# Fetching the rows of h: a second layout of x, a modulation copy by channel block, and earlier scores for one head pair

## The chip, the cores and the metric

The kernel runs on one core of a Trainium2 chip. The core has five engines with a queue of instructions each: TensorE (PE, with its weight loads shown as PEld), VectorE (DVE), ScalarE (ACT), GpSimd (POOL) and SyncE (SP). Each works through its own queue in order and waits on semaphores for the others. Sixteen DMA engines move data between DRAM and the on-chip memory (128 partitions); a DMA is issued by one of the engines, here mostly by SyncE, sometimes by GpSimd or ScalarE. The metric is the time of one launch in microseconds (us).

## The reference, cut to what matters

One layer of a backbone: 256 latent rows x and 256 context rows ctx, 2048 channels each. Both are normalised and modulated into h, and nearly all the rest are products of h with parts of one large matrix.

```python
mod = silu(c) @ w_mod + b_mod                 # shift, scale, gate; likewise for c_ctx
h   = layer_norm(x)   * (1 + scale)   + shift
h_c = layer_norm(ctx) * (1 + scale_c) + shift_c
aq, ak, av, az, bq, bk, bv, bz, bg, mga, mgb = split(h @ w_in)     # and the same for h_c
y_a = neighbourhood_attention(aq, ak, av, ak_c, av_c, na_rpb)       # 16 heads of 64
y_b = gated_linear_attention(bq, bk, bv, bg, and those of h_c)      # 4 heads, both directions
out = (sigmoid(mga) * ((y_a * silu(az)) @ w_br_a)
     + sigmoid(mgb) * ((y_b * silu(bz)) @ w_br_b)) @ w_out
x_new = layer_norm(alpha * x + gate * out, ln_g, ln_b)
```

The kernel never forms the values bv = h @ w_in[:, BV]. It multiplies the weights of the linear attention with the rows of h first (tile `g`) and then with that part of the matrix (tile `o`). For this it needs h with the rows on the partitions, beside the h with channels on the partitions that all other products use.

## The kernel before, in words

All products are done in a float32 form that TensorE takes at its fast rate: an operand is split into a high part (a cast on ScalarE, line 147) and a low part (a subtraction on VectorE, line 149), and three products are summed.

*Start (to about 136 us).* The rows of x and ctx are loaded, turned and normalised; the modulation is worked out per block of 128 channels (16 blocks, `mds`: scale and shift for latent and context), and h with channels on the partitions (`hhi`, `hlo`) is built block by block, together with the keys of the first seven head pairs (`kp`).

*The stream of weights.* All further weights come in units of 512 KB (352 KB for the value columns, `r_av`), in the order in which the program uses them. `load` issues the DMA on SyncE into one of four `raw` buffers, then ScalarE and VectorE split it. `load` also counts the units; a table `events` holds work that is tied to a count, and runs it as that load is written, ahead of the products of that unit. Thus the scores of the attention (`s`), the turning of its weights (`tp`) and the fetch of h rows are spread over the stream. `at(step, ...)` writes into that table.

*Attention.* `project_pair(p)` makes the keys and queries of head pair p; half of the low part of the queries is moved across partitions by a DMA that GpSimd issues (`q<-q`, line 488). `scores` multiplies them into the PSUM tile `s` (one pair of banks, so that the next scores wait until the exponentials have read it), adds the bias on VectorE (508), takes the maximum (510) and the exponentials on ScalarE (514). `read_values` (`op`) uses the result. Head pairs 0 to 5 go in groups of two, each followed by a third of the value columns (`va`, eight units); those take four PSUM banks, which the copies of the queries (483, 484, 487) have to free first. Head pair 6 is by itself: its two units are loads 37 and 38, the keys of pair 7 (`kp7`) are loads 39 and 40, its queries loads 41 and 42.

*Rows of h.* Eight blocks of 256 channels, block n at load 6 + 6n. `fetch_and_scale` issues on SyncE the modulation of the block to all partitions (`sb`, from the DRAM copy `mods`) and the four row groups of x and ctx (`xr`), and VectorE forms h from them (411, 412). One load later it is split, five loads later the two parts are stored to DRAM (`hrows`, line 425). `sb` and `xr` share two buffers (`staging`), so that a fetch waits for the stores of the block before to land; later two other tiles (`cs`, `wg`) use them as well, which is why the last block is fetched late. `mods` is written once by `store_modulation`, at about 136 us.

*The order.* Within an engine the framework's planner orders the instructions: by the order in which the program writes them, and by the time at which its own costs have their operands ready. `tc.issue_after(ins)` ties instructions behind another of the same engine.

*Later stages.* After the attention come keys, queries and gates of the linear attention (`bk`, `bq`, about 345 to 480 us), the `g` and `o` products that read `hrows` back (480 to 720), the gate `bz` with the gate column of the modulation (735 to 830), then `mga`, `pa`, `mgb`, `pb` (to 1140), the output product `wo`, and the last normalisation.

Of the kernel before, what the change touches and what calls it, by code (L numbers as in the profile page):

```python
# [8 lines left out]
F32 = mybir.dt.float32  # L9
# [7 lines left out]
P = 128  # L17
D = 2048
KT = 16
# [69 lines left out]
def tile_backbone_layer(  # L89
    ctx: ExitStack,  # L90
    tc: tile.TileContext,
    xin: bass.AP,
    cvec: bass.AP,
    wmod: bass.AP,
    bmod: bass.AP,
# [14 lines left out]
    nc = tc.nc  # L110
# [4 lines left out]
    small = ctx.enter_context(tc.tile_pool(name="small", bufs=4))  # L115
    ps = ctx.enter_context(tc.tile_pool(name="ps", bufs=1, space=PSUM))
    dram = ctx.enter_context(tc.tile_pool(name="dram", bufs=1, space=bass.MemoryType.DRAM))
    mods = dram.tile([2, 2, D], F32, name="mods")
    hrows = dram.tile([KT, P, 2, 4, P], F32, name="hrows")

    def k8(shape, name, dt=F32):
# [5 lines left out]
    def k2(shape, name, dt=F32):  # L127
        return work.tile(shape, dt, tag="k2", name=name, bufs=5)
# [7 lines left out]
    def bank(name):  # L136
        return ps.tile([P, 512], F32, tag="bank", name=name, bufs=2)

    def tiny(shape, name, bufs=4):
        return small.tile(shape, F32, tag=name, name=name, bufs=bufs)  # L140
# [4 lines left out]
    def split(hi, lo, src, after=None):  # L145
        with tc.issue_after(after[0]) if after else nullcontext():
            cast = nc.scalar.copy(hi, src)  # L147
        with tc.issue_after(after[1]) if after else nullcontext():
            sub = nc.vector.tensor_tensor(out=lo, in0=src, in1=hi.bitcast(F32), op=ALU.subtract)  # L149
        return cast.ins, sub.ins  # L150
# [79 lines left out]
    for i in range(4):  # L230
        cols = slice(P * i, P * i + P)
# [118 lines left out]
    for kt in range(KT):  # L350
# [3 lines left out]
        for p in range(K0):  # L354
# [3 lines left out]
            c = slice(P * p, P * p + P)  # L358
# [27 lines left out]
    def store_modulation():  # L386
        tp = bank("mdt")
        nc.tensor.transpose(tp[:64, :P], mds[:].rearrange("p a b k -> p (a b k)"), ident[:])
        mt = k2([64, P], "mdt")
        nc.vector.tensor_copy(mt[:], tp[:64, :P])  # L390
        nc.sync.dma_start(mods[:].rearrange("a b (k p) -> (a b k) p", p=P), mt[:])

    def staging(shape, name, dt=F32R):
        return const.tile(shape, dt, tag="staging", name=name, bufs=2)

    def rows_of_h(n):
        sb = staging([P, 2, 2, 256], f"sb{n}")
        xr = staging([P, 2, 4, P], f"xr{n}")
        b, x = sb[:].bitcast(F32), xr[:].bitcast(F32)
        cols = slice(256 * n, 256 * n + 256)  # L400

        def fetch_and_scale(dma, sub):
            with tc.issue_after(dma):
                nc.sync.dma_start(b, mods[:, :, cols].partition_broadcast(P))
                for i in range(4):
                    nc.sync.dma_start(x[:, :, i, :], xin[i, :, cols].rearrange("p (f c) -> p f c", f=2))
            for i in range(4):
                xi, s = x[:, :, i, :], i // 2
                scale, shift = (b[:, m, s, :].rearrange("p (f c) -> p f c", f=2) for m in range(2))
                with tc.issue_after(sub):  # L410
                    nc.vector.scalar_tensor_tensor(xi, xi, mvs[:, i, 0:1], scale, ALU.subtract, ALU.mult)
                nc.vector.scalar_tensor_tensor(xi, xi, rsn[:, 0, i : i + 1], shift, ALU.mult, ALU.add)

        def parts(dma, sub):
            with tc.issue_after(sub):
                split(
                    sb[:].rearrange("p a b c -> p (a b c)"),
                    xr[:].rearrange("p a b c -> p (a b c)"),
                    x.rearrange("p a b c -> p (a b c)"),
                )  # L420

        def store(dma, sub):
            with tc.issue_after(dma):
                for part, src in enumerate((b, x)):
                    nc.sync.dma_start(
                        hrows[2 * n : 2 * n + 2, :, part].rearrange("f p j c -> p f (j c)"),
                        src.rearrange("p f a b -> p f (a b)"),
                    )

        return fetch_and_scale, parts, store  # L430

    for n in range(8):
# [108 lines left out]
    def at(step, *calls):  # L541
        for fn, *args in calls:
            events.setdefault(step, []).append(lambda *_, fn=fn, args=args: fn(*args))
# [47 lines left out]
    for g in range(3):  # L591
        q = k8([P, 2, 2, 2, T], f"q{g}", F32R)
        first, second = project_pair(2 * g, q), project_pair(2 * g + 1, q)
        f0, s0, t0 = attention(2 * g, *first)
        f1, s1, t1 = attention(2 * g + 1, *second)
        n = len(loads) + 1
# [11 lines left out]
    f0, s0, t0 = attention(6, *first)  # L608
    f0()
    n = len(loads)  # L610
    at(n + 3, (s0, 0))
    at(n + 5, (s0, 1), (t0, 0))
    second = project_pair(7, q)
    f1, s1, t1 = attention(7, *second)
# [273 lines left out]
    for i in range(2):  # L888
        s = slice(4 * i, 4 * i + 4)
# [30 lines left out]
    def gate_b(c):  # L920
        z = rows_of(f"bz{c}", xh, xl, stepped=False)
        s = k4([P, 2, 512], f"sz{c}")
        yb = (yb0, yb1)[c // 2]
        for t in range(2):
            nc.scalar.activation(s[:, t, :], z[t][:], AF.Sigmoid)
            nc.vector.tensor_tensor(out=s[:, t, :], in0=s[:, t, :], in1=z[t][:], op=ALU.mult)
            y = yb[:, t, 512 * (c % 2) : 512 * (c % 2) + 512]
            nc.vector.tensor_tensor(out=s[:, t, :], in0=s[:, t, :], in1=y, op=ALU.mult)
        return s
# [48 lines left out]
    for c in range(NH):  # L978
        s = gate_b(c)
# [5 lines left out]
    for c in range(NC):  # L985
# [5 lines left out]
        sb, sig = gated(c, "b", ybh, ybl, KT)  # L991
# [46 lines left out]
    for g in range(NC - 1):  # L1038
        ops = [acc(f"wo{g}_{t}") for t in range(2)]
        for k in range(0, KT, 2):  # L1040
# [3 lines left out]
            for t in range(2):  # L1044
                for i in range(2):
                    c = slice(512 * i, 512 * i + 512)
# [68 lines left out]
    r, q = tiny([P, 1], "rr"), tiny([P, 1], "rt")  # L1115
# [14 lines left out]
    for g in range(NC):  # L1130
        cols = slice(512 * g, 512 * g + 512)
# [10 lines left out]
def _layout(inp):  # L1142
    import numpy as np

    a = {k: np.asarray(v) for k, v in inp.items()}
    f32 = np.float32
    r = {}
    r["xin"] = np.concatenate([a["x"][0].reshape(2, P, D), a["ctx"][0].reshape(2, P, D)])
    r["cvec"] = np.stack([a["c"][0].reshape(KT, P).T, a["c_ctx"].reshape(KT, P).T], axis=-1)

    wm, bm = a["w_mod"][0], a["b_mod"][0]
    cols = np.array([[D + P * k + np.arange(P), P * k + np.arange(P)] for k in range(KT)])
    w = wm.reshape(2, 8, P, 3 * D)
    r["wmod"] = np.stack([w[:, :, :, cols[k].ravel()].transpose(0, 2, 1, 3) for k in range(KT)])
    bsel = bm[cols].transpose(2, 0, 1)
    r["bmod"] = np.stack([bsel, bsel], axis=-1)
    r["wgate"] = wm[:, 2 * D :].reshape(KT, P, 2, 1024).transpose(0, 2, 1, 3)
    r["bgate"] = bm[2 * D :].reshape(1, D)

    win = a["w_in"][0]  # L1160
    r["wak"] = win[:, AK : AK + P * K0].reshape(KT, P, P * K0)
    av = np.concatenate([win[:, AV : AV + 1024], win[:, BG : BG + 32]], axis=1)
    av = av.reshape(8, 2, P, 3, AVW).transpose(3, 0, 2, 1, 4)
    r["wav"] = av.reshape(24, P, 2 * AVW)
    mats = {"w_in": win, "w_br_a": a["w_br_a"][0], "w_br_b": a["w_br_b"][0], "w_out": a["w_out"][0]}
    st = np.empty((len(UNITS), P, 1024), f32)
    for i, (_, (m, cl, k, n)) in enumerate(UNITS):
        blk = mats[m][P * k : P * (k + n)][:, cl]
        st[i] = blk.reshape(n, P, len(cl)).transpose(1, 0, 2).reshape(P, 1024)
    r["wst"] = st  # L1170

    pad = np.full((16, 15, 64, 64), NEG, f32)
    for c in range(64):
        c0 = min(max(c - 8, 0), 48)
        for kc in range(c0, c0 + 16):
            pad[:, :, c, kc] = a["na_rpb"][0][:, :, kc - c + 15]
    tab = np.empty((P, 16, 6, 64), f32)
    for rr in range(2):
        for e in range(6):
            tab[64 * rr : 64 * rr + 64, :, e, :] = pad[:, e - 2 - rr + 7].transpose(1, 0, 2)  # L1180
    r["rpb"] = tab.reshape(P, NP, 2, 384).transpose(1, 0, 2, 3)

    g2 = a["gla_w_gate2"][0]
    wg = np.zeros((4, 2, 16, 2, 512), f32)
    for d in range(2):
        wg[:, d, :, d, :] = g2[d]
    r["wg2"] = wg.reshape(P, 2, 512)
    r["bg2"] = a["gla_b_gate"][0].reshape(2, NH, P).transpose(2, 1, 0)
    r["ng"] = a["gla_norm_g"][0].reshape(4, P).T
    r["lng"] = a["ln_g"][0]  # L1190
    r["lnb"] = a["ln_b"][0]

    pos = np.arange(T)
    inv = 10000.0 ** (-np.arange(64, dtype=np.float64) / 64)
    inv = inv.astype(f32)
    ang = np.concatenate(
        [(pos // 64).astype(f32)[None, :] * inv[:, None], (pos % 64).astype(f32)[None, :] * inv[:, None]]
    ).astype(np.float64)
    r["rope"] = np.stack([np.cos(ang), -np.sin(ang), np.sin(ang)], axis=1).astype(f32)
    return {k: np.ascontiguousarray(v) for k, v in r.items()}  # L1200


_INS = [
    "xin", "cvec", "wmod", "bmod", "wgate", "bgate", "wak", "wav", "wst",
    "rpb", "wg2", "bg2", "ng", "lng", "lnb", "rope",
]

# [16 lines left out]
```

## Time and profile before

| | us |
|---|---|
| three runs | 1242.54, 1245.6, 1246.83 |
| median | 1245.6 |
| the profiled execution, its own time | 1247.71 |
| its span in the profile | 1246.0 |
| mean granted TensorE clock in it | 0.994 of full speed |
| sb fetches, median from issue to landing | 10.4 |
| xr fetches, median from issue to landing | 9.0 |
| loads of 352 KB (r_av), median from issue to landing | 4.5 |

The span is what the profiler sees of the program on the core; the profiled execution's own time has 1.7 us around it. A line like L404 is a line of the kernel before. A name as `sb<-mods` is the tile written and the one read; an "SPq" row is a DMA issue on SyncE, whose length is the time that SyncE was held by the issue, and not that of the transfer. In a row of a waits view, the bracket names how long the engine had stood still and who released it. In a windows row the columns are: stretch and length, busy time (and count) of PE, PEld, DVE, ACT and, where it worked, POOL, then the granted clock, the share of the DMA engines that was busy, and GB/s.

### The profile page before, as it was taken

To read this page: it belongs to the slowest core of one execution; us is meant where nothing else is said; L and a number is where in the kernel's file an instruction comes from. 1 tells how busy PE (TensorE), PEld (TensorE's weight loads), DVE (VectorE), ACT (ScalarE), POOL (GpSimd) and SP (SyncE) were. 2 spreads that over 40 slices of the span, in tenths; PEclk is the share of its full clock that TensorE was granted. 3 is DMA by queue.
4 is the path that set the end of the run, shared out by engine and by line. 5 is a ranking of instruction groups with operands and counts; after the bars stand their busy time and mean duration, and the time that the engine had idled before them with its cause. 6 is when DMAs were issued, how large, how long until landed. Compare 5 with 4: busy or idle time off the path is not lost.

```text
span 1246.0 us, 17116 instructions
## 1 busy us (share of the span) xinstructions
PE 1207.7 (97%) x6617; PEld 1015.1 (81%) x6617; DVE 757.5 (61%) x1114; ACT 536.9 (43%) x752; POOL 73.0 (6%) x106
## 2 busy tenths in 40 slices
PE   6999989999999999999999999999999999999997
PEld 5666889989788998888788898788888888888785
DVE  6755566666569376355543368898555554555577
ACT  4322445545456354253533364444444344444440
POOL 1000101010110101002000000000000000000111
PEclk9999989999999999999999999999999999999999
DMA  9997458787743434554645669989655556557661
GB/s 378 418 407 285 145 151 245 186 202 178 216 155 120 134 108 130 203 152 135 233 145 182 215 207 319 312 299 312 210 186 191 196 186 195 194 186 269 223 218 68
DMA packets 88993, 264.55 MB, mean 212 GB/s; under 512 B 9536, under 2 KB 22928, under 8 KB 83792
## 3 DMA queue, kind: packets, MB, share of 16 engines
q1 hardware_dynamic: 83744, 252.53, 60.3%
q0 software_dynamic: 4736, 10.37, 2.9%
q8 instruction: 52, 0.85, 0.3%
q10 hardware_dynamic: 432, 0.56, 0.1%
q14 instruction: 29, 0.24, 0.1%
HBM read 247.66 MB, written 10.52 MB: 207 GB/s over the span
## 4 chain that ended last, share of the span: by engine, by line
PE 70%; DMA 12%; DVE 10%; issue 3%; ACT 3%; SPq 2%; POOL 0%; DVEq 0%; ACTq 0%; POOLq 0%
PE bk L143 7%; PE mgb L143 7%; PE mga L143 7%; PE pb L143 7%; PE g L143 6%; PE o L143 6%; PE kp L143 6%; PE pa L143 3%; DMA wg<-in_wgate 3%; PE va L143 3%; PE bq L143 3%; PE wo L143 3%; PE az L143 2%; DMA hrows<-xr 2%; PE gp L143 2%
## 5 line engine op out<-in xcount | busy, mean ns | idle before, releaser
L149 DVE TENSOR_TENSOR l_wv<-r_wv,h_wv 128x1024 fp32r<-128x1024 f32 x32 | 39.2, 1225 | 79.8 <-ACT h_wv L147 79.6
L143 PE MATMUL o<-h_wv,gt 128*128 128x512 f32 x256 | 84.1, 391 | 0.6 <-DVE gt L149 0.6
L143 PE MATMUL g<-ah,hr 128*128 128x512 f32 x256 | 79.3, 390 | 1.1 <-DMA hr<-hrows 1.1
L143 PE MATMUL va<-h_av,hhi 128*128 128x352 f32 x192 | 64.5, 336 | 9.9 <-ACT q L487 9.9
L149 DVE TENSOR_TENSOR l_pb<-r_pb,h_pb 128x1024 fp32r<-128x1024 f32 x32 | 39.2, 1225 | 47.8 <-ACT h_pb L147 47.8
L147 ACT CAST h_wv<-r_wv 128x1024 fp32r<-128x1024 f32 x32 | 33.6, 1049 | 74.4 <-DMA r_wv<-in_wst 74.4
L143 PE MATMUL va<-h_av,hlo 128*128 128x352 f32 x192 | 63.0, 328 | 0.0
L143 PE MATMUL va<-l_av,hhi 128*128 128x352 f32 x192 | 62.9, 327 | 0.0
L149 DVE TENSOR_TENSOR l_mgb<-r_mgb,h_mgb 128x1024 fp32r<-128x1024 f32 x32 | 39.2, 1224 | 32.7 <-ACT h_mgb L147 32.5
L955 DVE SCALAR_TENSOR_TENSOR gacc<-wg,sc,gacc 128x512 f32<-128x512 f32 x64 | 46.4, 747 | 17.9 <-DMA wg<-in_wgate 17.5
L143 PEld LDWEIGHTS o<-h_wv,gt 128*128 128x128 f32 x256 | 47.8, 188 | 11.6 <-DVE gt L149 1.8
L149 DVE TENSOR_TENSOR l_mga<-r_mga,h_mga 128x1024 fp32r<-128x1024 f32 x32 | 39.1, 1223 | 28.9 <-ACT h_mga L147 28.9
L143 PEld LDWEIGHTS g<-ah,hr 128*128 128x128 f32 x256 | 47.7, 188 | 11.0 <-DMA hr<-hrows 1.3
L147 ACT CAST h_mga<-r_mga 128x1024 fp32r<-128x1024 f32 x32 | 33.8, 1055 | 49.5 <-PE mga L143 31.2
L143 PE MATMUL kp<-hhi,h_ak 128*128 128x512 f32 x128 | 52.7, 418 | 2.2 <-ACT hhi L304 2.2
L147 ACT CAST h_mgb<-r_mgb 128x1024 fp32r<-128x1024 f32 x32 | 33.6, 1054 | 47.7 <-PE mgb L143 26.1
L147 ACT CAST h_pb<-r_pb 128x1024 fp32r<-128x1024 f32 x32 | 33.7, 1053 | 43.4 <-PE pb L143 30.1
L143 PE MATMUL bz<-l_bz,hhi 128*128 128x512 f32 x128 | 50.1, 391 | 2.0 <-DVE l_bz L149 2.0
L143 PE MATMUL kp<-hhi,l_ak 128*128 128x512 f32 x128 | 51.7, 404 | 0.0
L304 ACT ACTIVATE hhi<-xt,mds 128x256 fp32r<-128x256 f32 x32 | 17.5, 594 | 78.8 <-DVE mds L298 78.8
L143 PE MATMUL bk<-hhi,h_bk 128*128 128x512 f32 x128 | 50.4, 394 | 0.7 <-ACT kf L675 0.7
L143 PE MATMUL kp<-hlo,h_ak 128*128 128x512 f32 x128 | 50.6, 398 | 0.0
(351 smaller groups left out, 3560.4 us busy)
## 6 DMA issues: line engine op xcount, KB each, us to landing
wm<-in_wmod SPq DMA_DIRECT2D x32, 1024.0 KB, 9.4
hr<-hrows SPq DMA_DIRECT2D x32, 512.0 KB, 4.3
r_wv<-in_wst SPq DMA_DIRECT2D x32, 512.0 KB, 3.6
r_bz<-in_wst SPq DMA_DIRECT2D x32, 512.0 KB, 4.9
wg<-in_wgate SPq DMA_DIRECT2D x64, 256.0 KB, 5.1
r_mga<-in_wst SPq DMA_DIRECT2D x32, 512.0 KB, 3.6
r_mgb<-in_wst SPq DMA_DIRECT2D x32, 512.0 KB, 3.3
r_pb<-in_wst SPq DMA_DIRECT2D x32, 512.0 KB, 3.3
```

The costliest lines, as they stand in the source:

```text
L143: return nc.tensor.matmul(o, a, b, start=start, stop=stop).ins
L147: cast = nc.scalar.copy(hi, src)
L149: sub = nc.vector.tensor_tensor(out=lo, in0=src, in1=hi.bitcast(F32), op=ALU.subtract)
L304: cast = nc.scalar.activation(hhi[:, s, kt, :], x, AF.Identity, scale=m, bias=b)
L955: nc.vector.scalar_tensor_tensor(part, raw[:], sc[:, n // 4, 0:1], part, ALU.mult, ALU.add)
```

## The change

Three things. First, the host hands over x and ctx a second time, as `xrow`: for each block n and each partition, the four row groups' 2 x 128 channels lie in one piece of 4 KB. The four xr DMAs of a block, which read 512 B pieces, become one. Second, the modulation copy in DRAM has the channel block outermost, (16, 4, 128) in place of (2, 2, 2048). So the scale and shift of a block of 256 channels, for latent and context, are one run of 4 KB in place of four of 1 KB; `sb` has the same order on chip, and the operands of lines 411 and 412 are cut accordingly. The store of that copy is issued by GpSimd and not by SyncE. Third, the first scores of head pair 6 are tied to load 40 in place of load 41.

```diff
-    mods = dram.tile([2, 2, D], F32, name="mods")
+    mods = dram.tile([KT, 4, P], F32, name="mods")
...
         nc.vector.tensor_copy(mt[:], tp[:64, :P])
-        nc.sync.dma_start(mods[:].rearrange("a b (k p) -> (a b k) p", p=P), mt[:])
+        nc.gpsimd.dma_start(mods[:].rearrange("k a p -> a k p"), mt[:])
...
     def rows_of_h(n):
-        sb = staging([P, 2, 2, 256], f"sb{n}")
+        sb = staging([P, 2, 4, P], f"sb{n}")
         xr = staging([P, 2, 4, P], f"xr{n}")
         b, x = sb[:].bitcast(F32), xr[:].bitcast(F32)
-        cols = slice(256 * n, 256 * n + 256)
 
         def fetch_and_scale(dma, sub):
             with tc.issue_after(dma):
-                nc.sync.dma_start(b, mods[:, :, cols].partition_broadcast(P))
-                for i in range(4):
-                    nc.sync.dma_start(x[:, :, i, :], xin[i, :, cols].rearrange("p (f c) -> p f c", f=2))
+                nc.sync.dma_start(b, mods[2 * n : 2 * n + 2].partition_broadcast(P))
+                nc.sync.dma_start(x, xrow[n])
             for i in range(4):
                 xi, s = x[:, :, i, :], i // 2
-                scale, shift = (b[:, m, s, :].rearrange("p (f c) -> p f c", f=2) for m in range(2))
+                scale, shift = (b[:, :, 2 * m + s, :] for m in range(2))
...
     f0()
     n = len(loads)
-    at(n + 3, (s0, 0))
+    at(n + 2, (s0, 0))
     at(n + 5, (s0, 1), (t0, 0))
...
     r["xin"] = np.concatenate([a["x"][0].reshape(2, P, D), a["ctx"][0].reshape(2, P, D)])
+    r["xrow"] = r["xin"].reshape(4, P, 8, 2, P).transpose(2, 1, 3, 0, 4)
```

More of the change, by code (lines that the diff above doesn't have):

```diff
@@ L92, in tile_backbone_layer @@
     xin: bass.AP,
+    xrow: bass.AP,
     cvec: bass.AP,
@@ L1203 @@
 _INS = [
-    "xin", "cvec", "wmod", "bmod", "wgate", "bgate", "wak", "wav", "wst",
+    "xin", "xrow", "cvec", "wmod", "bmod", "wgate", "bgate", "wak", "wav", "wst",
     "rpb", "wg2", "bg2", "ng", "lng", "lnb", "rope",
```

## The prediction, made before the result was known

> **What bounds the kernel now.** I read the page first, then the busy time of each engine by stage, then TensorE's waits, the chain of waits around them, SyncE's issues, and last the traffic in single stretches.
>
> ```profile
> PE 1207.7 (97%) x6617; PEld 1015.1 (81%) x6617; DVE 757.5 (61%) x1114; ACT 536.9 (43%) x752; POOL 73.0 (6%) x106
> PE 70%; DMA 12%; DVE 10%; issue 3%; ACT 3%; SPq 2%; POOL 0%; DVEq 0%; ACTq 0%; POOLq 0%
> ```
>
> TensorE sets the end: it is busy for 97% of the span, and no other engine is near it. Seen over the whole, only what lets TensorE stand still, or run slower, can be won. The change touches the rows of h, whose eight blocks are fetched between 144 and 587 us. In that part TensorE stands still only in a few places (windows; columns are PE, PEld, DVE, ACT, POOL busy with counts, granted clock, DMA share, GB/s):
>
> ```profile
> 222.00:345.00 123.00, 117.75 (x773) 109.70 (x772) 77.69 (x126) 59.74 (x110) 12.23 (x24) 0.99 0.75 196
> 345.00:480.00 135.00, 133.92 (x824) 118.49 (x823) 89.82 (x168) 65.49 (x103) 17.47 (x20) 1.00 0.40 129
> ...
> 155.70:160.87 5.17, 0.01 (x1) 0.00 (x0) 4.13 (x11) 1.91 (x4) 0.68 (x2) 0.91 0.63 214
> 160.87:167.70 6.83, 6.83 (x24) 6.44 (x25) 4.71 (x6) 2.06 (x3) 0.34 (x1) 0.56 0.33 80
> 216.97:219.00 2.03, 0.02 (x1) 0.00 (x0) 1.42 (x5) 1.83 (x5) 0.67 (x2) 1.00 0.22 53
> 272.50:275.20 2.70, 0.03 (x2) 0.01 (x1) 2.12 (x7) 2.29 (x5) 0.69 (x2) 1.00 0.26 80
> 275.20:278.60 3.40, 3.40 (x12) 3.03 (x13) 3.06 (x5) 2.18 (x3) 0.33 (x1) 0.62 0.51 132
> 339.20:341.80 2.60, 0.03 (x1) 0.04 (x1) 1.02 (x2) 1.53 (x5) 0.00 (x0) 1.00 1.31 277
> ```
>
> Four stops, which I call A (5.2 us), B (2.0), C (2.7) and D (2.6). After A and C the granted clock is 0.56 and 0.62 for a while, so those stops cost more than their length: (1 - 0.56) x 6.83 = 3.0 us after A and (1 - 0.62) x 3.40 = 1.3 us after C. Behind 345 us TensorE is full again. So the most that can be won here is 5.2 + 3.0 + 2.0 + 2.7 + 1.3 + 2.6 = 16.8 us.
>
> The chain of waits says who ends A, B and C (start, length, what):
>
> ```profile
> 150.51 7.79 DMA r_av<-in_wav
> ...
> 158.38 0.78 ACT h_av L147
> ...
> 160.44 0.39 ACT q L487
> ...
> 209.05 7.39 DMA r_av<-in_wav
> ...
> 265.37 7.25 DMA r_av<-in_wav
> ```
>
> The weight tile that lands at 158.3 is cast on ScalarE, and behind that cast on the same engine stand the copies of q that free the PSUM banks for the value columns. From landing to TensorE's restart it takes 160.87 - 158.30 = about 2.5 us, and the same in B and C. A weight load of this size lands late because it is the first one behind a fetch of h rows. SyncE's own rows show it:
>
> ```profile
> 135.86 0.51 SPq L391 DMA_DIRECT2D mods<-mdt  x1
> ...
> 144.57 0.44 SPq L404 DMA_DIRECT2D sb<-mods  x1
> 145.06 5.36 SPq L406 DMA_DIRECT2D xr<-in_xin  x4
> 150.51 2.67 SPq L156 DMA_DIRECT2D r_av<-in_wav  x3
> ...
> 204.82 4.19 SPq L406 DMA_DIRECT2D xr<-in_xin  x4
> ...
> 259.56 0.36 SPq L404 DMA_DIRECT2D sb<-mods  x1
> 260.81 4.51 SPq L406 DMA_DIRECT2D xr<-in_xin  x4
> ```
>
> SyncE is held 4.2 to 5.4 us in the four xr issues, and only then sends the load. And the transfers themselves are slow:
>
> ```profile
> 147.50:153.50 6.00, 6.00 (x51) 6.00 (x50) 2.63 (x4) 2.97 (x6) 1.03 (x2) 1.00 0.33 107
> 321.00:325.00 4.00, 4.00 (x20) 3.30 (x19) 0.56 (x1) 1.35 (x2) 0.51 (x1) 1.00 0.44 92
> ...
> 587.50:589.50 2.00, 2.00 (x10) 1.68 (x9) 1.20 (x4) 1.49 (x2) 0.00 (x0) 1.00 0.78 220
> 317.00:319.00 2.00, 2.00 (x13) 1.78 (x13) 0.42 (x1) 1.15 (x2) 0.03 (x1) 1.00 1.07 410
> ...
> 1146.50:1154.00 7.50, 7.50 (x35) 6.21 (x34) 2.45 (x2) 3.10 (x3) 0.00 (x0) 1.00 1.01 419
> ```
>
> In the first two stretches sb is read: 512 KB to 128 partitions, for each partition the same four pieces of 1 KB that lie 8 KB apart in DRAM. It runs at 92 to 107 GB/s with the DMA engines a third busy, so 512 KB takes 5 us or more. The xr pieces of 512 B, alone at 587.5, run at 220 GB/s. Loads and stores in pieces of 2 KB and more run at 410 (317 to 319 us), and so does the stretch in which lng and lnb go to all partitions beside weight loads, another read of one place by 128 partitions, but 8 KB in one piece: 419 GB/s.
>
> **The change part by part.**
>
> *x and sb fetch (lines 404 to 406).* Removed: per block three of four xr issues. Bytes stay at 512 KB each. Added: nothing.
>
> ```profile
> L406 SPq DMA_DIRECT2D xr<-in_xin x32: 372/877/2341, 145.1 to 587.4; - x32
> L404 SPq DMA_DIRECT2D sb<-mods x8: 359/360/440, 144.6 to 545.0; - x8
> r_pb<-in_wst SPq DMA_DIRECT2D x32, 512.0 KB, 3.3
> bgt<-in_bg POOLq DMA_DIRECT2D x1, 4.0 KB, 5.7
> ```
>
> One issue should take near the shortest seen, 0.37 us, in place of 4.2 to 5.4 per block: SyncE reaches the next load some 4 to 5 us sooner. For the transfers the bounds are: sb no faster than now (about 100 GB/s), or as fast as the lng rows (419). I take full rate, since the new piece is one contiguous 4 KB like the lng row's 8 KB, and the form it leaves, four 1 KB pieces, is the only slow one. xr, 4 KB per partition like every weight load, goes at 410. Then sb and xr are 1.05 MB at 410 GB/s, 2.6 us, and the 352 KB of r_av 0.9 us; with 1 us to complete, 4.5 us from the first byte (the 1 us is an estimate: r_pb, 512 KB, lands 3.3 us after its issue, its bytes take 1.3, and half of the other 2.0 comes after them). In A the first byte of sb comes at about 147 us (estimate: 2.4 us behind its issue, when the low-rate stretch begins), so r_av lands at 151.5 instead of 158.3. TensorE stops at 155.70 and needs 2.5 us: 153.2 is soon enough. A is gone with 1.7 us to spare; I keep 0.8 us for a raw buffer that comes free later. B: TensorE stops at 216.97, so 214.4 is soon enough; r_av is sent at about 205.3 and lands near 210. C: 270.0 is soon enough; sent at 261.3, it lands near 266.5. With A and C go their low clocks. A: -(5.2 + 3.0 - 0.8) = -7.4; B: -2.0; C: -(2.7 + 1.3) = -4.0 us.
>
> The Trainium skill, page "DMA: Bandwidth & Descriptors", section Specifications, says that pieces of 512 B and more already run at line rate. The 220 GB/s of the 512 B pieces beside the 410 of the larger ones disagree by almost a factor of two, though both stretches are short. By that rule longer pieces bring no faster transfer at all, and the sum would be that of the first rival below.
>
> *Modulation copy (line 391).* Its issue (0.51 us) moves from SyncE to GpSimd, where the copies of kh wait for ScalarE until 140 anyway. A small GpSimd-issued transfer lands in 5.7 us (bgt above); 135.9 + 0.5 + 5.7 = 142.1 is still ahead of the first reader at 144.57. What is next on SyncE, rb of pair 0, waits for its buffer in any case. Cost 0, bounds 0 to +1 us; if that cover went, sb0 would be late by the difference.
>
> *Scale and shift (lines 411, 412).* The same 64 VectorE instructions over the same elements; in1 is now two runs of 128 like in0. Cost 0; in0 has that form already. If it cost 0.05 us each (a tenth of their 0.48), 3 us of VectorE, a 61% busy engine, would hide most.
>
> *Last block (585.96).* There the four parts are used as they land:
>
> ```profile
> 585.96 1.92 SPq L406 DMA_DIRECT2D xr<-in_xin  x4
> ...
> 589.25 0.48 DVE L411 SCALAR_TENSOR_TENSOR xr<-xr,mvs,sb 128x256 f32<-128x256 f32 x1 [0.77 <-DMA xr<-in_xin]
> ```
>
> VectorE starts on the first part 3.3 us after its issue. One transfer of 512 KB lands as late as that (r_pb, 3.3), so VectorE starts as before and then never waits for the other three. Cost 0, bounds -1 to +1.
>
> *Scores of pair 6 (line 611).* They move from load 41 to load 40, so on TensorE from behind all of kp7 (two units) to behind its first unit. Before the change:
>
> ```profile
> 329.26 0.91 DVE L411 SCALAR_TENSOR_TENSOR xr<-xr,mvs,sb 128x256 f32<-128x256 f32 x2 [3.60 <-DMA xr<-in_xin]
> ...
> 338.21 0.70 DVE L508 TENSOR_TENSOR s<-s,rb 128x512 f32<-128x512 f32 x1
> ...
> 341.77 1.21 PE L143 MATMUL s<-kh,q 128*128 128x512 f32 x4 [2.58 <-ACT pr L514]
> ...
> 321.18 0.51 POOL L488 DMA_DIRECT2D q<-q  x1 [1.70 <-DVE q L484]
> ...
> 317.65:328.72 11.07, 11.07 (x48) 8.83 (x48) 0.00 (x0) 0.00 (x0) 1.00 0.72 224
> ...
> DMA to landing us min/median/max: 8.1/8.1/8.1
> ```
>
> D comes from VectorE: it waits for xr at 329.26, so the bias of the first scores is added only at 338.21, and the second scores (341.77) wait for the first's exponentials, which free the PSUM pair. With xr some 5 us sooner and the scores earlier, D's 2.6 us go. But the earlier place has a new wait: kp7's first unit ends at 317.65 + 11.07 / 2 = 323.2, and the q that the scores read was sent at 321.18 and landed 8.1 us later, at 329.3. In TensorE's order all of kp7's second unit and qp7 would stand behind it. That wait lies between 0 (the planner puts the scores further back) and 6.1 us. The old 8.1 us were in the worst of the sb traffic; that traffic should be over sooner, but q has 1.8 us to the place where it is read and the fastest case would still be some 2 us late, and the planner may put it back: I take 1.5, nearer to 0. D: -2.6 + 1.5 = -1.1 us.
>
> Sum: -7.4 - 2.0 - 4.0 - 1.1 = -14.5 us. The profiled execution took 1247.7 us (span 1246.0 and 1.7 around it), so it would be 1233.2; it was 2.1 us above the median of 1245.6, so for the median I say 1231.
>
> **The rivals.**
>
> *The place is slow, not the pieces.* All 128 partitions still read one 4 KB place, and sb stays at 100 GB/s. For: the DMA engines were a third busy, so they waited on the source. Against: lng at 419. Then only SyncE's time and xr's rate are won: from the first byte 5.2 + 1.3 + 0.9 + 1 = 8.4 us. A: lands at 155.4, 2.2 us stay and the low clock too, -3.0; B: 213.2, gone, -2.0; C: 269.4, just gone, -4.0; D -1.1. Sum -10.1: 1235.5.
>
> *The moved scores hold TensorE.* q lands as late as now: D becomes -2.6 + 6.1, with a low clock as after A 3.0 more, so +6.5 beside -13.4: -6.9, 1238.7. For: the 8.1 us. Against: it takes the planner's order to be the written one.
>
> *The place gets hotter: slower than before.* The four places become one; if that halves the rate to 50 GB/s, sb takes 10.5 us and r_av in A lands at 147 + 10.5 + 3.2 = 160.7 instead of 158.3. The other fetches are late by as much, four stops x 2.4 = +9.6: 1255. It decides from the point where sb takes 158.3 - 147 - 3.2 = 8.1 us, 65 GB/s. For: the third-busy engines. Against: lng again, and SyncE's 4 us.
>
> *Nothing is left.* The order of every engine is planned anew from changed transfers; a worse order later gives the gain back, about 1244. For: the last block's sb is issued at 545.0 (L404 row), far behind the 48th load, to which the code ties it, so the planner does move things. Against: behind 345 us TensorE has little left to lose its place to.
>
> **How the numbers follow.** Forecast 0.58, with its own range 1227 (all 16.8 won, and 2 us of scatter) to 1236; slow place 0.19; held scores 0.09; nothing left 0.07; hotter place 0.07. A measurement of this kernel can tell about 0.3%, 3.7 us, from no change. The first three are all faster: 0.86; within 0.07; slower 0.07. The range 1226 to 1243 holds the first three with their bounds and leaves out the last two.
>
> **What would show it.** xr issued once in about 0.4 us; no stop of TensorE at A, B, C, and a clock near 1 behind them; the DMA rate during sb near 400 GB/s (100: first rival; under 65: third); the first scores of pair 6 preceded by a wait for q (second rival). Wrong if r_av behind a fetch still lands 7 us after its issue, or if TensorE shows new stops of over 2 us between 136 and 345 us.

## The result, and the profile after

The changed kernel takes 1233.74 us (median of four runs, 1232.27 to 1234.71) against 1244.93 us for the kernel before on the same chip (median of four runs; three of them gave the 1245.6 above): a ratio of 0.991, with a 95% interval of 0.989 to 0.9931. Its profiled execution took 1233.74 us, with a span of 1232.0 us (before: 1247.71 and 1246.0). In the changed kernel the scale and shift lines are L410 and L411, sb and xr are issued in L404 and L405, and the copies of q stand in L482, L483, L486 and L487.

From the page after, busy time of the engines, and the chain that ended last by engine:

```profile
PE 1203.8 (98%) x6617; PEld 1013.1 (82%) x6617; DVE 758.0 (62%) x1114; ACT 538.6 (44%) x752; POOL 73.4 (6%) x107
...
PE 83%; DVE 8%; DMA 4%; issue 2%; ACT 2%; POOL 1%; SPq 0%; DVEq 0%; ACTq 0%; POOLq 0%
```

TensorE's busy time fell by 1207.7 - 1203.8 = 3.9 us, and its standing time from 38.3 to 28.2 us, by 10.1; together these are the 14.0 us. The share of DMA in the chain fell from 12 to 4%.

The stretch of the fetches, 136 to 345 us, first before, then after (windows; columns as in the prediction):

```profile
136.00:345.00 209.00, 196.55 (x1291) 183.99 (x1292) 132.00 (x212) 101.17 (x184) 24.54 (x48) 0.98 0.72 195
```

```profile
136.00:345.00 209.00, 202.92 (x1328) 188.92 (x1329) 138.09 (x219) 107.38 (x194) 26.40 (x51) 0.98 0.69 210
...
155.66:157.81 2.15, 0.08 (x1) 0.00 (x1) 2.07 (x6) 1.14 (x3) 0.69 (x2) 1.00 0.16 33
157.81:164.00 6.19, 6.19 (x37) 6.02 (x38) 4.70 (x6) 2.88 (x5) 0.34 (x1) 1.00 0.48 134
216.00:220.00 4.00, 4.00 (x27) 4.00 (x26) 1.59 (x4) 2.74 (x6) 0.00 (x0) 1.00 0.15 56
271.00:276.00 5.00, 5.00 (x34) 4.78 (x33) 2.48 (x5) 2.44 (x4) 0.00 (x0) 1.00 0.50 146
310.59:315.62 5.03, 1.09 (x4) 0.34 (x3) 0.00 (x0) 1.04 (x1) 0.00 (x0) 0.87 0.63 239
315.62:321.10 5.48, 5.47 (x13) 4.32 (x14) 4.64 (x8) 1.45 (x4) 0.00 (x0) 0.50 0.27 75
147.50:149.50 2.00, 2.00 (x19) 2.00 (x19) 1.65 (x3) 1.46 (x4) 0.52 (x1) 1.00 0.79 311
```

TensorE stood still for 209 - 196.55 = 12.5 us before and for 6.1 after. Row by row: of A, 2.1 us stay, with a full clock behind them; B and C are gone (216 to 220 and 271 to 276 are full, at clock 1.00); and at 310.6 to 315.6 there is a stop of 5.03 - 1.09 = 3.9 us that was not there before, with the clock at 0.50 for the next 5.5 us. The last row shows the stretch in which sb is read: 311 GB/s, where the kernel before had 105 in the same two microseconds. A second execution of the changed kernel has 269 there, so the rate is some 2.6 to 3 times the old one, and below 400.

TensorE's waits in the same stretch (releaser; us in total, times, longest), after:

```profile
PE s L144 <- DMA q<-q: 3.9, 2, 2.9
PE va L144 <- ACT q L486: 2.1, 1, 2.1
...
```

The chain of waits around both (start, length, what), after:

```profile
145.11 8.35 DMA xr<-in_xrow
...
153.56 0.88 DVE xr L410 x2
154.44 0.79 DVE xr L411 x2
155.24 0.40 DVE xr L410
...
155.66 0.43 DVE q L483
...
157.38 0.39 ACT q L486
...
157.81 1.22 PE va L144 x6
...
306.45 0.51 POOL q L487
...
308.66 6.83 DMA q<-q
...
315.62 0.76 PE s L144
```

What is left of A has two causes, one close behind the other. The last to release TensorE is VectorE: it has to copy q out of the PSUM banks that the value columns need, and that copy (155.66) stands in its queue behind five operations on xr, which wait for the one transfer of x. But the weight tile behind the fetch is late too:

```profile
L157 SPq DMA_DIRECT2D r_av<-in_wav x1: 328/328/328, 146.6 to 146.6; - x1
...
DMA to landing us min/median/max: 8.1/8.1/8.1
```

SyncE sends it 3.9 us sooner than before (146.6 against 150.5), and it lands 8.1 us later, at 154.7 (before: 158.3). From such a landing to TensorE's restart it takes about 2.5 us, as before, so with VectorE out of the way TensorE could have started at 157.2; it started at 157.8. By this estimate 1.5 of the 2.1 us are the weight tile's and 0.6 VectorE's.

The new stop is the moved scores: the second part of q is sent at 308.66 and lands 6.83 us later. TensorE has no other work in its order before these scores; it waits 1.0 us for the first part of q and 2.9 for the second, and goes on at 315.62.

SyncE's rows (issue in ns, least/median/most), and the median landing times, after:

```profile
L404 SPq DMA_DIRECT2D sb<-mods x8: 326/332/458, 144.6 to 536.6; - x8
L405 SPq DMA_DIRECT2D xr<-in_xrow x8: 328/332/447, 145.1 to 577.5; - x8
```

```profile
sb<-mods SPq DMA_DIRECT2D x8, 512.0 KB, 5.6
xr<-in_xrow SPq DMA_DIRECT2D x8, 512.0 KB, 6.1
q<-q POOLq DMA_DIRECT2D x16, 64.0 KB, 4.8
```

sb lands in 5.6 us (10.4 before), x in 6.1 (9.0), and SyncE is held 0.33 us for x where it was held 4.2 to 5.4.

So between 136 and 345 us the kernel won 12.5 - 6.1 = 6.4 us of standing, and on the low clock (3.0 + 1.3) - (1 - 0.50) x 5.48 = 1.6 us: 8.0 of the 14.0 by which the two profiled executions differ. The other 6.0 came later. About 3 of them are scatter: the profiled execution of the kernel before was 2.8 us above its median, and by the medians the kernel won 11.2 us. TensorE's waits behind 345 us show two that the profile after lacks. Before:

```profile
PE bz L143 <- DVE l_bz L149: 2.0, 2, 1.3
...
PE g L143 <- DMA hr<-hrows: 1.1, 1, 1.1
```

It is tempting to book these 3.1 us to the fetches, as the last block's sb is issued at 536.6 in place of 545.0. The run with only the scores moved (below) speaks against it: its fetches are the old slow ones, and the two waits are 0.2 us each. What came behind 345 us stays open.

### The profile page after: what moved, and what is told of

It reads as the page before. It is cut to its first block, busy times and chain, and to the rows that moved or that the text cites. A ratio compares the mean times of both kernels' runs of the same rounds, so it can differ in the third digit from the quotient of the medians.

```text
span 1232.0 us, 17106 instructions
## 1 busy us (share of the span) xinstructions
PE 1203.8 (98%) x6617; PEld 1013.1 (82%) x6617; DVE 758.0 (62%) x1114; ACT 538.6 (44%) x752; POOL 73.4 (6%) x107
## 4 chain that ended last, share of the span: by engine, by line
PE 83%; DVE 8%; DMA 4%; issue 2%; ACT 2%; POOL 1%; SPq 0%; DVEq 0%; ACTq 0%; POOLq 0%
PE bk L144 7%; PE bz L144 7%; PE mgb L144 7%; PE mga L144 7%; PE pb L144 7%; PE o L144 7%; PE kp L144 7%; PE g L144 6%; PE va L144 6%; PE pa L144 4%; PE wo L144 3%; PE az L144 3%; PE qp L144 2%; PE gp L144 2%; PE bq L144 2%
## 5 line engine op out<-in xcount | busy, mean ns | idle before, releaser
L148 ACT CAST h_bz<-r_bz 128x1024 fp32r<-128x1024 f32 x32 | 33.7, 1054 | 39.5 <-PE bz L144 35.3
```

## The experiments

The kernel before took 1244.3, 1247.7 and 1250.0 us on the three chips used here, so each ratio is to the kernel before on the same chip. Four theories stood at the start: the moved scores cost what TensorE waits for q; the gain comes from sb; it comes from x in one transfer; the order is only planned otherwise.

**The scores back in their old place.** The changed kernel, with one line undone:

```diff
-    at(n + 2, (s0, 0))
+    at(n + 3, (s0, 0))
```

> The changed kernel, with the first scores of head pair 6 tied to load 41 again. Theory (held scores): in the changed kernel TensorE stands in front of these scores until q lands, 5.6 us and 2.3 us of low clock behind it; with the scores back in their place both go, and of the old stop D (2.6 us) at most 1 us returns, since xr lands sooner. So about 6 us less than the changed kernel: 1227.7. Rival (the forecast's step): the move is worth 1.1 us, so about 1235.

Measured: 1229.77 us, ratio 0.9842 (0.9824 to 0.986). Windows of this kernel:

```profile
136.00:345.00 209.00, 206.67 (x1362) 192.91 (x1363) 141.91 (x224) 110.61 (x201) 27.99 (x52) 1.00 0.71 215
...
339.00:342.00 3.00, 3.00 (x19) 2.58 (x18) 2.21 (x3) 2.02 (x3) 0.50 (x1) 1.00 0.44 176
```

Of 209 us TensorE stands still for 2.3, and the place of D is full too (339 to 342): with x and sb early, D goes without any move of the scores. By the medians the move was a loss of about 4 us, from two chips, and of 4.4 to 5.1 us on one chip below (the changed kernel once more beside two kernels with the scores back), though the stop and its low clock alone are 3.9 + 2.7 = 6.6 us in the profile. The theory had the cause, and about 2 us too much: its 5.6 us of standing were 3.9 by the waits. Without the move the kernel beats both.

**Only the scores moved.** The kernel before, with the same line changed the other way.

> The kernel before, with nothing but the first scores of head pair 6 tied to load 40. Theory (held scores): q lands 8.1 us after its issue among the old traffic, so TensorE stands some 6 us in front of them, with a low clock of 2 to 3 us behind, against the 2.6 us of D: about 6 us slower than before, 1251. Rival: the move removes D and costs 1.5 us, 1243.8.

Measured: 1252.05 us, ratio 1.002 (1.0001 to 1.0039), 2.1 us slower by the medians. TensorE's waits:

```profile
PE va L143 <- ACT q L487: 8.8, 3, 4.3
PE s L143 <- DMA q<-q: 6.5, 1, 6.5
```

The wait for q is there, 6.5 us, near the 6.1 that the prediction named as the upper bound, and D is gone. The direction is as expected, the size is not: of the 6.5 - 2.6 = 3.9 us between the two stops about half reaches the end by the medians. Behind 345 us the two waits named above have shrunk in this kernel, by 2.7 us together:

```profile
PE g L143 <- DMA hr<-hrows: 0.2, 1, 0.2
...
PE bz L143 <- DVE l_bz L149: 0.2, 1, 0.2
```

That may be where part of it is regained; one profile of each kernel can't tell it from scatter.

**sb from the old copy, x in one piece.** The kernel with the scores back, and the old layout of the copy (four pieces of 1 KB, 8 KB apart).

```diff
-    mods = dram.tile([KT, 4, P], F32, name="mods")
+    mods = dram.tile([2, 2, D], F32, name="mods")
...
-                nc.sync.dma_start(b, mods[2 * n : 2 * n + 2].partition_broadcast(P))
+                nc.sync.dma_start(b, mods[:, :, cols].partition_broadcast(P))
```

> The run e1_scores_back with the old order of the modulation copy: sb again reads four pieces of 1 KB, 8 KB apart; x comes in one piece of 4 KB. Theory (the form of sb is what made the fetch slow): sb runs at about 100 GB/s, the load behind a fetch lands some 4 us later than in e1, the stops at A and perhaps C come back: 4 to 6 us more than e1, about 1233. Rival (the many small pieces of x made it slow): same time as e1, within 1 us.

Measured: 1251.51 us, ratio 1.0017 (1.0005 to 1.003). All of the gain is gone, 22 us in all beside the kernel with the scores back. Its waits, a window behind the first fetch, and its chain:

```profile
PE va L144 <- ACT q L487: 13.1, 3, 5.7
```

```profile
148.00:154.00 6.00, 6.00 (x50) 6.00 (x49) 2.44 (x4) 2.75 (x6) 1.03 (x2) 1.00 0.99 99
```

```profile
145.34 11.98 DMA xr<-in_xrow
```

The rate is 99 GB/s again, now with the DMA engines 99% busy, and x behind it lands 12 us after its issue. In one piece it can be used only when all of it is there, which may be why this kernel is even a little slower than the one before. The loss is far larger than the 4 to 6 us expected: TensorE stands still for 14.0 us between 136 and 345 us, against 2.3 with the scores back, and behind that a wait of scores for the exponentials takes another 4.7. TensorE, VectorE, ScalarE and GpSimd execute the same instructions in the same order in both kernels, so the gain hangs on sb.

**x as before, sb new.** The kernel with the scores back, and the four old x transfers of 512 B pieces.

```diff
...
-                nc.sync.dma_start(x, xrow[n])
+                for i in range(4):
+                    nc.sync.dma_start(x[:, :, i, :], xin[i, :, cols].rearrange("p (f c) -> p f c", f=2))
```

> The run e1_scores_back with the four old transfers of x in pieces of 512 B; sb reads 4 KB in one piece. Theory (the form of sb is what made the fetch slow, and SyncE was held by sb's slow drain): the four issues take about 0.4 us each, 1.5 us together, xr lands 1 to 2 us later than in e1: 0 to 2 us more than e1, about 1229. Rival (the pieces of x): SyncE held 4 us per block again and xr late, 5 us or more above e1, 1233.

Measured: 1229.39 us, ratio 0.9838 (0.9818 to 0.9857), the same as with x in one piece. SyncE's row, a window, and a wait:

```profile
L407 SPq DMA_DIRECT2D xr<-in_xin x32: 378/468/559, 144.8 to 569.7; - x32
```

```profile
148.00:154.00 6.00, 6.00 (x49) 6.00 (x48) 4.63 (x10) 3.03 (x6) 1.03 (x2) 1.00 0.99 298
```

```profile
PE va L144 <- ACT q L488: 0.3, 1, 0.3
```

The second layout of x brings nothing. Four issues take 4 x 0.47 = 1.9 us, not 4.2 to 5.4: SyncE had been held by the slow sb in front, not by the x transfers. VectorE can start on the first part of x while the others travel, and of A 0.3 us stay here. But the weight tile also landed sooner in this execution (at 153.1, against 154.8 with the scores back), and A's rest varies: 0.2 to 2.1 us with x in one piece, 0.3 to 1.3 with x in four. No gain of the four parts is shown.

**The changed kernel once more**, on the chip of the next three.

> The changed kernel once more, on the chip of this group, so that the others stand beside it. By the first timing 0.991 of the kernel before; if the gain of e1_scores_back over it is real and not one of the chip, it stays near 0.991 here, about 0.7% above e1.

Measured: 1234.19 us, ratio 0.9888 (0.9867 to 0.9909). The wait for q is there again (3.1 us). A's rest is 0.2 us this time: x landed at 151.3 and the weight tile at 152.6, where they had come at 153.5 and 154.7.

**Is it the length of the pieces or their distance?** Two kernels, both with the scores back and x in one piece. In the first the pieces of 1 KB stay four, but lie 9 KB apart in place of 8; in the second they lie 1.25 KB apart (and the copy is stored by four transfers in place of one).

```diff
# first, against the kernel before: rows of 9 KB
-    mods = dram.tile([2, 2, D], F32, name="mods")
+    mods = dram.tile([2, 2, D + 256], F32, name="mods")
...
# second, against the changed kernel: [block, 4, 256 of 320]
-    mods = dram.tile([KT, 4, P], F32, name="mods")
+    mods = dram.tile([8, 4, 320], F32, name="mods")
...
```

> The run e3_sb_old with one number changed: the rows of the modulation copy are padded by 1 KB, so that the four 1 KB pieces of sb lie 9 KB apart and not 8 KB. Theory (the distance: pieces 8 KB apart fall on one place of the DRAM): sb is fast, the time is that of e1, 0.984 of before. Rival (the size: a read of one place by 128 partitions is slow in 1 KB pieces): sb stays near 100 GB/s, the time is that of e3, 1.00 of before.

> The run e1_scores_back with sb read in four pieces of 1 KB that lie 1.25 KB apart, so nearly in one run of 5 KB (the copy is stored by four transfers instead of one). Theory (the distance of 8 KB): fast, 0.984 of before. Rival (the size of 1 KB): slow as e3, 1.00 of before. If this one is fast and e6 slow, it is the nearness and not the aliasing of 8 KB that counts.

Measured: 1229.78 us, ratio 0.9847 (0.9821 to 0.9873), and 1229.05 us, 0.9844 (0.9827 to 0.9861). The window behind the first fetch, at 9 KB and then at 1.25 KB:

```profile
148.00:154.00 6.00, 6.00 (x50) 6.00 (x49) 2.70 (x5) 2.69 (x6) 1.03 (x2) 1.00 0.95 311
```

```profile
148.00:154.00 6.00, 6.00 (x49) 6.00 (x48) 2.93 (x5) 2.24 (x5) 1.02 (x2) 1.00 0.97 322
```

Pieces of 1 KB are as good as one of 4 KB, and the kernel with rows of 9 KB differs from the slow one in nothing but 1 KB of distance (TensorE, VectorE, ScalarE and GpSimd execute the same instructions in the same order): 311 GB/s against 99, 21.7 us of the whole by the two medians, which are from two chips. It is the distance.

**The fetch a load later.** The kernel with the scores back; fetch, split and store of each block one load later, so that A's rest would have more room.

```diff
-        events.setdefault(6 + 6 * n, []).append(lambda dma, sub, n=n: rows_event(n, dma, sub))
+        events.setdefault(7 + 6 * n, []).append(lambda dma, sub, n=n: rows_event(n, dma, sub))
...
-        events.setdefault(7 + 6 * n, []).insert(0, parts)
-        events.setdefault(11 + 6 * n, []).insert(0, store)
+        events.setdefault(8 + 6 * n, []).insert(0, parts)
+        events.setdefault(12 + 6 * n, []).insert(0, store)
```

> The run e1_scores_back with every block of h rows fetched, split and stored one load later. Theory: the 2.1 us that are left of stop A come from VectorE, which waits for the first block's xr in front of the q of pair 1; one load later that q is through: about 2 us less than e1, 0.9825 of before. Rival: the stop only moves to a later place, same as e1 within 1 us.

Measured: 1239.22 us, ratio 0.9928 (0.9911 to 0.9945): a miss. A's rest is gone, but the last block's x is sent at 581.5 (570.7 with the scores back). SyncE's row, a window, and the chain there:

```profile
L405 SPq DMA_DIRECT2D xr<-in_xrow x8: 328/333/922, 147.9 to 581.5; - x8
```

```profile
573.00:594.00 21.00, 11.09 (x40) 9.16 (x41) 15.07 (x40) 4.90 (x10) 0.53 (x1) 0.67 0.64 231
```

```profile
578.16 3.29 DMA hrows<-xr
...
581.47 0.35 SPq L405
...
581.87 6.27 DMA hr<-hrows
...
588.27 5.04 PE g L144 x12
```

TensorE stands still for 9.9 of 21 us, and the clock is 0.67 on the mean. The last x can go out only when the store of the block before has landed and left its buffer (578.16 + 3.29), and the read of stored rows that the `g` products need stands behind it in SyncE's queue; TensorE waits 4.8 us for that read, and 5.1 for VectorE, which has work on xr in front of what TensorE needs next. The fetch has no room behind it: all blocks share two buffers, with other tiles too.

**One number in the kernel before.** The kernel before with rows of 9 KB in the copy; x, the scores and the issuing engine as they were.

```diff
-    mods = dram.tile([2, 2, D], F32, name="mods")
+    mods = dram.tile([2, 2, D + 256], F32, name="mods")
...
-        nc.sync.dma_start(mods[:].rearrange("a b (k p) -> (a b k) p", p=P), mt[:])
+        nc.sync.dma_start(mods[:, :, :D].rearrange("a b (k p) -> (a b) k p", p=P), mt[:])
```

> The kernel before with one thing changed: the rows of the modulation copy in DRAM are padded by 1 KB, so that the four pieces of sb lie 9 KB apart. Old x fetch in four transfers, store on SyncE, scores of pair 6 in their old place. Theory (the distance of 8 KB is all of it): the time of e1 and e4, 0.984 of before. Rival (the second layout of x or the move of the store adds to it): between 0.987 and 0.991.

Measured: 1229.08 us, ratio 0.988 (0.9863 to 0.9896); the kernel before took 1244.32 on this chip. A window, SyncE's row, and the landing of sb:

```profile
136.00:345.00 209.00, 207.47 (x1366) 193.60 (x1367) 142.10 (x226) 110.95 (x202) 26.87 (x51) 1.00 0.71 215
```

```profile
L406 SPq DMA_DIRECT2D xr<-in_xin x32: 372/468/569, 145.2 to 571.1; - x32
```

```profile
sb<-mods SPq DMA_DIRECT2D x8, 512.0 KB, 5.3
```

TensorE stands still for 1.5 us of 209; 1.2 of them are what is left of A, and that now begins with the weight tile:

```profile
147.52 7.08 DMA r_av<-in_wav
```

TensorE, VectorE, ScalarE and GpSimd execute the same instructions in the same order as in the kernel before, so a new order has no part in it. This is the simplest version, and it beats both kernels.

The gain depends on the chip, and that lies with the kernel before: it takes 1244.3, 1247.7 and 1250.0 us on the three chips, while the kernels with a fast sb, the scores in their old place and the fetch at its old load take 1229.1 to 1229.8 on all of them. So the fast sb is worth 15 to 21 us. Why the slow one costs more on one chip than on another was not settled.

**How much distance is enough?** The same edit with 64 and with 128 extra columns: rows of 8.25 KB and of 8.5 KB.

> As e9_pad1k with a padding of 256 B. If the rate of sb goes with how many different addresses within 8 KB the four pieces cover (1 KB without padding at about 100 GB/s, 4 KB with 1 KB of padding), 256 B covers 1.75 KB: about 175 GB/s, some 3 us for sb, and about half of the gain, 0.992. Rival (any padding that breaks the exact 8 KB is enough): the full gain, 0.984. Other rival (it takes a whole piece of padding): no gain, 1.00.

> As e9_pad1k with a padding of 512 B, which covers 2.5 KB of different addresses within 8 KB: by that theory about 250 GB/s, 2.1 us for sb, and nearly the full gain, 0.986. Any padding is enough: 0.984. A whole piece of padding is needed: 1.00.

Measured: 1242.99 us, ratio 0.9987 (0.9972 to 1.0002), and 1229.43 us, 0.9877 (0.9863 to 0.9892). With 8.25 KB, a window and the landing:

```profile
148.00:154.00 6.00, 6.00 (x50) 6.00 (x49) 2.21 (x3) 2.31 (x6) 1.02 (x2) 1.00 0.89 134
```

```profile
sb<-mods SPq DMA_DIRECT2D x8, 512.0 KB, 10.0
```

With 8.5 KB:

```profile
148.00:154.00 6.00, 6.00 (x50) 6.00 (x50) 4.21 (x9) 2.76 (x6) 1.02 (x2) 1.00 0.94 277
```

```profile
sb<-mods SPq DMA_DIRECT2D x8, 512.0 KB, 6.9
```

256 B more bring almost nothing, 512 B all of it. None of the three theories on record fits both: the one that counts different addresses had half of the gain and then nearly all, the second (any padding) all at both, the third (a whole piece) none at both. In these six microseconds the rate rises with the padding (104 GB/s before, then 134, 277, and 288 with 9 KB); the time makes one step, somewhere between 256 and 512 B. What in the memory makes the distance count was not tried and stays open. The Trainium skill, page "DMA: Bandwidth & Descriptors", section "Latency and other measured facts", reports that copies slow down when the rows of the partitions lie at large powers of two in DRAM, that some KB of padding restores them and 192 B does not, and calls the cause an inference. These runs agree in kind; they show it at 8 KB, where the page's distances begin at 512 KiB, and 512 B as enough. The page's distances go from partition to partition; here they lie within the read that all partitions share.

## Why the prediction was right, and where it was not

The sign was right, and the time nearly (1231 forecast, 1233.7 measured; profiled 1233.2 forecast, 1233.7 measured). The sum is nearer than its terms: between 136 and 345 us 14.5 were forecast and 8.0 won, and 6.0 us came where none was forecast. That this nearly made up the difference is luck.

*What bounds the kernel.* Right for the stretch. Its 16.8 us are about what a fast fetch wins there: the kernel before with rows of 9 KB stands still for 1.5 us, at clock 1.00, and is 15.2 us faster on its chip. As the most that could be won it was too low, as the 20 us and more on another chip show; and "Behind 345 us TensorE is full again" holds to 480 only. From 480 to 840 us TensorE stood still for 5.0 us in that profile.

*x and sb fetch.* That sb would be fast was right: 311 and 269 GB/s in the stretch of sb. The two rivals of a slow and a hotter place, 100 and below, both fall. SyncE's 0.33 us was right. The size was not. The load behind the fetch was to land 4.5 us after the first byte, at 151.5; it landed at 154.7, after 7.7. The sum counted sb, xr and that load, 1.41 MB at 410 GB/s. The six microseconds from 148 moved 1.9 MB at 322 GB/s: a lower rate, and more bytes, as two more loads were sent by 152 us. Nor was the reason right. "The form it leaves, four 1 KB pieces, is the only slow one": four pieces of 1 KB are fast at 9, 8.5 and 1.25 KB of distance. The rows before held both a length and a distance, and the prediction compared only lengths.

*The rate of xr and SyncE's hold.* Both were booked as things that x in one piece would mend. The hold came from the slow sb in front: with it gone, the four issues take 1.9 us, x in pieces of 512 B lands after 4.1 and 4.2 us by the median (9.0 before), and the second layout is worth nothing. Of the 220 GB/s at 587.5 us, set against the rule of the Trainium skill on pieces of 512 B and more (page "DMA: Bandwidth & Descriptors", section "Specifications"), less is known. With x in 512 B pieces the six microseconds from 148 run at 298 GB/s, and at 311 and 322 with x in one piece of 4 KB: close, as the rule would have it. But the last block's x in 512 B pieces still runs at 222 GB/s with the slow sb gone (the kernel before with rows of 9 KB, 571.2 to 573.2 us), and no stretch holds x alone in pieces of 4 KB, so there the runs do not decide. In the time no cost of the short pieces shows.

*A.* Forecast -7.4, measured -(5.2 + 3.0 - 2.1) = -6.1. The step that failed is the landing at 151.5: 153.2 was soon enough for the weight tile, and 154.7 was 1.5 us too late. And "153.2 is soon enough" followed r_av alone. VectorE's copy of q stands behind its work on xr, and that had to wait for all of x: another 0.6.

*B and C.* Forecast -2.0 and -4.0. Right: both stretches are full, and the clock is 1.00. The loads there took 7.5 and 7.1 us from their issue, not about 5, but had the room.

*D.* Forecast -2.6 + 1.5 = -1.1, measured -2.6 + 3.9 + 2.7 = +4.0 (2.7 = half of 5.48 us at clock 0.50). The step that failed is "the planner may put it back: I take 1.5, nearer to 0". The planner left the scores where they were written, and q took 6.83 us to land; the prediction's own fastest case, some 2 us late, was already more than the 1.5. The second rival had the step right (+6.5 with its low clock); its total of 1238.7 was too long for want of the gains behind 345 us. And the -2.6 needed no move: it came with sb.

*Modulation copy, scale and shift.* Forecast 0. The copy lands 2.9 us after GpSimd's issue at 136.2, and no reader waits for it; the 64 VectorE operations take 478 and 480 ns by the median, as before. Right.

*Last block and after.* The last block was put at 0, and nothing was forecast behind 345 us. The profiles differ by 6.0 us there, nearly the errors in A (1.3) and D (5.1). About 3 us of that are scatter of the profiled executions, and no run ties the rest to the change.

*The signs.* Two of the signs of being wrong came. One is the new stop before the scores, 3.9 us in all, with the second rival's wait for q. The other, that r_av still lands 7 us after its issue, was badly chosen. At A, B and C the load lands 8.1, 7.5 and 7.1 us after its issue, no sooner than before; but SyncE sends it sooner, and counted from the issue of sb in front it lands after 10.1, 9.2 and 8.8 us, where it took 13.7, 12.7 and 13.1.

## What to carry to other kernels

When a transfer is slow, list what its pieces differ in from a fast one, length, number and distance, before one of them is called the cause; padding the rows of a DRAM tile by 512 B or 1 KB is an edit of two lines, and here it gave all that a new layout gave. An issue that holds its engine, or a slow transfer, may only stand behind another slow one. A forecast of a landing has to count every transfer that is under way beside it. Before a product is moved forward, compare the landing time of its latest operand with the work that stays in front of it; here 6.8 us of transfer stood against some 2 us of work.

## What the runs showed of the hardware

- Reading four pieces of 1 KB into 128 partitions alike, with the pieces 8 KB apart in DRAM, ran at about 100 GB/s (99 in one kernel, 104 and 107 in two stretches of another). The six microseconds behind the first fetch ran at 134 with 8.25 KB, at 277 with 8.5 KB, at 288 with 9 KB. The DMA engines were a third busy in one kernel and 99% busy in another at the same slow rate, so that share does not tell a slow source from a full queue.
- GpSimd's copy of 64 KB between partitions (q) took 6.83 us to land while the DMA engines were 73% busy, against a median of 4.8.
- TensorE's stop of 2.1 us left the clock at 1.00. Two stops of 1.0 and 2.9 us, with two products between them, were followed by a clock of 0.50 for 5.5 us.
